# Gated rows that move into the places of the up projection's forms

## The chip, the cores and the metric

The kernel runs on one NeuronCore of a Trainium2 chip. The metric is the device time of one execution in microseconds; the kernel before takes 1738.56 us (median of 3 runs, 1738.2 to 1738.58). One execution was also recorded by the hardware profiler; every row below is from that one.

The engines are named as in the profile: PE is the matrix engine (PEld its weight loads), DVE the vector engine, ACT the scalar engine, POOL the general-purpose engine, and SP the queue that issues all DMA transfers here. Each engine works through its own list of instructions in order; semaphores tie the lists together.

## The reference

One step of a decoder layer is computed for 1024 prompt tokens and for 8 requests of 8 sample tokens, in float32: an RG-LRU branch and an S5 branch, merged, and then a ConvFFN. Only the ConvFFN bears on the change:

```python
h = modulate(x, p['g_norm2'], sh2, sc2)
up = h @ p['w_up']                              # 1024 -> 6144
uc, new_ffn_conv = causal_dwconv(ffn_conv, up, p['ffn_conv_w'], p['ffn_conv_b'])   # 3 taps
ua, ub = jnp.split(uc, 2, axis=-1)
x = x + gt2[:, None] * ((jax.nn.gelu(ua) * ub) @ p['w_down'])                      # 3072 -> 1024
```

## The kernel before

Channels lie on the 128 partitions, tokens along the free dimension. The tokens are in two halves: half 0 has the 64 sample tokens and 512 prompt tokens (576 columns), half 1 the other 512. Every operand of a float32 product is split into two parts that the matrix engine takes: the high part is a copy by ACT into the rounded type fp32r, the low part is a subtraction by DVE (value minus high part). A product is then three matmuls: high by high, high weight by low row, low weight by high row.

**The up projection** (`up`, L1451) takes the 6144 output channels in 12 column pairs b = 0 to 11, each with a part 0 (the gelu argument) and a part 1 (the factor). For each of these 24 steps a `Quad` makes seven block products `p1` to `p7` in place of eight, after Strassen and Winograd. Their moving operands are the *forms* B11, B21, B22, T1 to T4: sums and differences of the blocks of h, four tiles each, split once ahead of the loop and kept in SBUF for all 24 steps. B11, B21, T2, T4 and B22 lie in the 20 places P0 to P19 of the pool `pairs` (the table `FORMS` at L1133 gives the places), T1 and T3 in the pool `forms`. Product `p1` reads B11, `p2` B21, `p3` B22, `p4` T4, `p5` T1, `p6` T2 and `p7` T3. A step runs p1, then p4 of the step before it (`pend`), p5, p6, p2, p3, p7; the p4 of the last step comes after the loop. In the rows, L1238 is a product with 288-column matmuls (p1, p2, p6, p4), L1234 one with 512 columns (p3, p5), L1241 is p7.

A product leaves PSUM through `evac` (L1393 on ACT for p4, L1398 on DVE for p2, p3 and p7). When both halves of 128 channels are there, `finish` does the convolution: `fix` moves the carried columns on POOL (L1364 to L1369), L1374 (ACT) and two L1376 (DVE) are the three taps, L1483 multiplies prompt columns by the gelu and L1481 does the same for the 64 sample columns on POOL (tile `cs`). SP stores both to the DRAM tiles `act0` and `act1` (L1482, L1484).

**The down projection** follows. `down_a` (half 0) loads all 24 gated row blocks back with `load_act`: SP loads one into a buffer `al` (L1493), ACT and DVE split it into the tile `act` (L1147, L1148). Then `strip` goes over four strips of 256 output channels. In each, `weights` loads 12 pieces of `w_down` (L192), each split on ACT and DVE (L175, L176), and each piece meets two row blocks in 24 matmuls (L223). `down_b` does the same for half 1 (L1531).

**Buffers.** `al` shares the tag `cp` (five buffers) with `t1`, `p5` and `u2`, PSUM results of a Quad that wait for their second operand. Split weights `wh` and `wl` have three buffers each, raw weights eight. The `act` tiles are in a pool of 28 buffers that is opened only when the pools of the up projection, `pairs` among them, are closed; it takes over their memory, so that a first write to an `act` tile waits for whatever last used that memory.

**Order.** A scheduler orders the instructions of each engine by the program's order and by priorities. Code under `tc.high_priority(offset=n)` counts as n places earlier. SP issues in its own list's order: a transfer that waits holds back all behind it.

Of the kernel before, what the change touches and what calls it, by code (L numbers as in the profile page):

```python
# [8 lines left out]
F32 = mybir.dt.float32  # L9
F32R = mybir.dt.float32r  # L10
# [40 lines left out]
def _body(ctx, nc, tc, a):  # L51
# [4 lines left out]
    pairs = ctx.enter_context(ExitStack())  # L56
    pp = pairs.enter_context(tc.tile_pool(name="pairs", bufs=1))
    phase = ctx.enter_context(ExitStack())

    def pool(name, bufs=1):  # L60
        return phase.enter_context(tc.tile_pool(name=name, bufs=bufs, reuse_waits="tile"))
# [32 lines left out]
    def slot(i, name, dt=F32R):  # L94
        return pp.tile([128, 2, 576], dt, tag=f"P{i}", name=name)
# [5 lines left out]
    WID = (576, 512)  # L101
# [55 lines left out]
    def rg(name):  # L157
        return tmp("rg", [128, 604], name, bufs=4 if two else 7)
# [181 lines left out]
    def new_acc(name):  # L340
        return tmp("acc", [128, 512], name, bufs=1)
# [787 lines left out]
    actd = [dp.tile([24, 128, WID[h]], F32, name=f"act{h}") for h in range(2)]  # L1129
# [3 lines left out]
    FORMS = dict(B11=(12, 14, 8, 10), B21=(13, 15, 9, 11), T2=(0, 1, 2, 3), T4=(4, 5, 6, 7), B22=(16, 17, 18, 19))  # L1133
# [12 lines left out]
    def split_form(x, f):  # L1146
        S.activation(x[:, 0], f, AF.Copy)  # L1147
        V.tensor_sub(x[:, 1], f, x[:, 0].bitcast(F32))  # L1148
# [127 lines left out]
    def cpt(name):  # L1276
        return uw.tile([128, 576], F32, tag="cp", name=name, bufs=5)

    def blocks_of(w):
        q = Blocks(w)  # L1280
        with tc.high_priority(offset=300):
            q.load("A11", "A21", "A22", "A12")
            q.sums(V)
        return q
# [98 lines left out]
    def evac_up(b, part, gl):  # L1383
        m0 = 24 * part + 2 * b
        raw = {}

        def evac(i, half, y, z, e=None):
            t = tmp("rx", [128, 656], "up", bufs=5)
            o = t[:, 32:544] if half else t[:, :576]
            o = halves(o) if len(y.shape) == 3 else o  # L1390
            with tc.high_priority(offset=1000):
                if z is None:
                    S.activation(o, y, AF.Copy)  # L1393
                elif e is not None:
                    V.tensor_sub(o, y, z)
                    V.tensor_add(o, o, e)
                else:
                    V.tensor_add(o, y, z)  # L1398
            raw[i, half] = t
            if (i, 1 - half) in raw:  # L1400
                finish(i, raw, part, m0 + i, gl, 2 * b + i)

        return evac

    def up_lead():

        nonlocal rB2
        gl = {}
        Q = [Quad(q, evac_up(0, i, gl)) for i, q in enumerate(lead)]
        x = slot512(2, "wx")  # L1410
        Q.append(Quad(Blocks(a["w_up"][12], (("A11", x[:, 0]), ("A12", x[:, 1]))), evac_up(0, 1, gl)))
        Q[1].q.load("A11", "A12")
        Q[0].p1()
        rB2 = slot(3, "rstdB2", F32)[:, 0, :512]
        with tc.high_priority(offset=200):
            rstd_from(acc2, 512, "rstdB2", out=rB2)
            ST = h2b_load()
        Q[0].p2()
        Q[1].p1()
        Q[1].p2()  # L1420
        e = mm("e")
        ada_tail()
        h2b(ST)
        Q[0].p3_first(e[:, 0])
        with tc.high_priority(offset=300):
            Q[1].q.load("A21", "A22")
            Q[1].q.sums(G)
        Q[0].p5_last()
        Q[1].p3_first(e[:, 1])
        Q[1].p5_last()  # L1430
        for q in Q:
            q.p6()
            q.c12()
        for q in Q:
            q.p7()
        Q[0].p4()
        return Q[1]
# [13 lines left out]
    def up():  # L1451
        pend = up_lead()
        for b in range(1, 12):
            gl = {}
            for part in range(2):
                q = Quad(blocks_of(a["w_up"][12 * part + b]), evac_up(b, part, gl))
                q.p1()
                pend.p4()
                q.p5()
                q.p6()  # L1460
                q.p2()
                q.p3()
                q.p7()
                pend = q
        pend.p4()

    def finish(i, raw, part, m, gl, k):
        for half in range(2):
# [15 lines left out]
            nc.sync.dma_start(actd[half][k][:, 512 * half - 512:] if half else actd[0][k][:, 64:576], u[:, :512])  # L1484


    def load_act(half, k):
        n = WID[half]
        x = pp.tile([128, 2, 576], F32R, tag="act", name=f"act{half}_{k}", bufs=28)[:, :, :n]

        with tc.high_priority(offset=150 if half == 0 and k < 2 else 0):
            t = cpt("al")[:, :n]
            nc.sync.dma_start(t, actd[half][k])  # L1493
            split_form(x, t)
        return x

    def down_a():
        act = [load_act(0, k) for k in range(24)]
        acc3 = new_acc("acc3A")
        for b in range(4):  # L1500
            acc = strip(0, a["w_down"], b, act, 24)
            for j in range(2):
                m = 2 * b + j
                d = x2d[0][m * 128:(m + 1) * 128]
                x = load_x(d, "x2r")
                xo = rg("xo")[:, :512]
                with tc.high_priority(offset=400):
                    for y, c0, c1 in acc[j].p:
                        V.scalar_tensor_tensor(xo[:, c0:c1], y, modT[:, 40 + m, 0:1], x[:, c0:c1],
                                               op0=OP.mult, op1=OP.add)  # L1510
                resid_s(acc[j], 40 + m)
                acc_sq(acc3, xo, m == 0)
                nc.sync.dma_start(d, xo)
        hot.append(final(0, acc3, None, 0))

    def down_b():

        act = [load_act(1, k) for k in range(24)]
        X3 = [pp.tile([128, 2, 576], F32, tag="act", name=f"x3_{i}", bufs=28).rearrange("p r x -> p (r x)")[
            :, :1024].rearrange("p (r x) -> p r x", r=2) for i in range(4)]  # L1520
        acc3 = tmp("accb", [128, 512], "acc3B", bufs=1)
        CUT = 18

        def rows_of(T, b, k0, k1, tok):
            for i, (hi, lo) in enumerate(weights(a["w_down"], b, range(k0 // 2, k1 // 2))):
                for m in range(2):
                    c = slice(m * 128, (m + 1) * 128)
                    for k in range(2):
                        kb = k0 + 2 * i + k
                        for n, (y, r) in enumerate(((hi, 0), (hi, 1), (lo, 0))):  # L1530
                            T_.matmul(T[:, m, tok], y[:, k, c], act[kb][:, r, tok], start=kb + n == 0,  # L1531
                                      stop=kb == 23 and n == 2, skip_group_check=True)
                tick()

        def out(T, b, tok):
            for j in range(2):
                m = 2 * b + j
                x = load_x(x2d[1][m * 128:(m + 1) * 128, tok], "x2r")
                xo = X3[b][:, j, tok]
                with tc.high_priority(offset=400):  # L1540
                    V.scalar_tensor_tensor(xo, T[:, j, tok], modT[:, 40 + m, 0:1], x, op0=OP.mult, op1=OP.add)
                if b < 3:
                    acc_sq(acc3[:, tok], xo, m == 0)
                else:
                    sq.append(rg("sq")[:, tok])
                    S.activation(sq[-1], xo, AF.Square)
            if b < 3:
                scale_gf(X3[b][:, :, tok], b)

        def scale_gf(x, b):  # L1550
            for j in range(2):
                S.activation(x[:, j], x[:, j], AF.Copy, scale=v("gf")[:, 2 * b + j:2 * b + j + 1])

        whole = slice(0, 512)
        T = [mm("mm")]
        rows_of(T[0], 0, 0, 24, whole)
        out(T[0], 0, whole)
        for b in range(1, 4):
            T.append(mm("mm"))
            rows_of(T[b], b, 0, CUT, whole)  # L1560
        for t in range(2):
            tok = slice(256 * t, 256 * t + 256)
            sq = [acc3[:, tok]]
            for b in range(1, 4):
                rows_of(T[b], b, CUT, 24, tok)
                out(T[b], b, tok)
            g = final(1, sq, [x[:, :, tok] for x in X3], 512 + 256 * t, scale_gf)
            if t == 0:
                hot.append(g)
            else:  # L1570
                drain(g)
# [73 lines left out]
    ph = pool("forms")  # L1645
    tp = pool("up", 2)
    rB2 = None
    up()
    nc.sync.dma_start(a["o_sfc"], fconv)
    nc.sync.dma_start(a["o_pfc"], fcarry)  # L1650
    phase.close()
    pairs.close()

    pp = pool("act")
    tp, ph = pool("tmp2", 2), pool("part2")
    two = True
    down_a()
    down_b()


# [147 lines left out]
```

## Time and profile before

| | |
|---|---|
| median of 3 runs | 1738.56 us (1738.2 to 1738.58) |
| the profiled execution | 1742.4 us, its span 1740.6 us |
| PE busy | 1688.3 us, 97% of the span |
| DVE, ACT, POOL busy | 1198.6, 878.0, 220.7 us |
| granted TensorE clock, mean | 0.988 of full speed |
| HBM traffic | 143 GB/s over the span |

The span is the time from the first to the last instruction of the core; the rest of the profiled time lies around it. PE is busy almost throughout, so a place where it is idle, or where its clock is lowered, is time that the end of the program sees. The places are found by cutting the span into short windows, and then by the list of instructions in order of time in such a window, where each row says how long its engine was idle before it and what released it. The step from the up to the down projection lies between 1414 and 1440 us.

### The profile page before, as it was taken

How to read it: one execution, taken by the hardware profiler on the slowest of the kernel's cores; microseconds unless marked ns; L12 is line 12 of the kernel's file. 1: busy time of each engine (PE TensorE's matmuls, PEld its weight loads, DVE VectorE, ACT ScalarE, POOL GpSimd, SP SyncE). 2: the span in 40 equal slices, each digit the busy share in tenths (PEclk: the TensorE clock that was granted, in tenths of full speed). 3: DMA queues.
4: the chain of work that ended last, by engine and by line, in shares of the span. 5: the costliest groups of instructions: out<-in, count | busy, mean ns of one | idle time of the engine just before them, and what ended most of it. 6: DMA issues, size and time to landing. Idle time of an engine off the chain costs nothing.

```text
span 1740.6 us, 29344 instructions
## 1 busy us (share of the span) xinstructions
PE 1688.3 (97%) x10654; PEld 1521.1 (87%) x10654; DVE 1198.6 (69%) x2559; ACT 878.0 (50%) x1539; POOL 220.7 (13%) x488
## 2 busy tenths in 40 slices
PE   6999999999999999999998999999999989999997
PEld 2999999999997877788777999999999979999887
DVE  8878688956745686666669877777777766336426
ACT  4557668424534476744446555555555545234224
POOL 0012110100000001020021323322222230000000
PEclk8999999999999999999998999999999999999999
DMA  8375333467646655455662322222222249345634
GB/s 304 106 239 163 101 117 126 123 181 214 196 132 202 206 173 155 135 158 181 202 223 68 91 77 75 75 75 75 76 75 76 80 131 298 122 136 174 193 97 134
DMA packets 158993, 250.85 MB, mean 144 GB/s; under 512 B 34049, under 2 KB 57601, under 8 KB 158849
## 3 DMA queue, kind: packets, MB, share of 16 engines
q1 hardware_dynamic: 158848, 248.99, 45.8%
q8 instruction: 83, 1.36, 0.3%
q14 instruction: 62, 0.50, 0.1%
HBM read 205.20 MB, written 43.73 MB: 143 GB/s over the span
## 4 chain that ended last, share of the span: by engine, by line
PE 71%; DVE 6%; DMA 2%; ACT 1%; issue 1%; POOLq 0%; SPq 0%; POOL 0%; DVEq 0%; ACTq 0%
PE mm L225 15%; PE mm L223 15%; PE b L1238 13%; PE e L1234 8%; PE mm L1531 7%; PE a L1238 4%; PE b L1241 3%; PE sada L268 1%; DMA al<-act 1%; DVE wlo L176 1%; PE pv L777 1%; PE pg L951 1%; PE prs L347 0%; PE sx L707 0%; PE sx L708 0%
## 5 line engine op out<-in xcount | busy, mean ns | idle before, releaser
L176 DVE TENSOR_TENSOR wlo<-raw,whi 128x512 fp32r<-128x512 f32 x240 | 165.2, 688 | 163.9 <-ACT whi L175 131.2
L175 ACT ACTIVATE whi<-raw 128x512 fp32r<-128x512 f32 x240 | 150.6, 627 | 242.9 <-PE mm L225 101.5
L223 PE MATMUL mm<-h1A,whi 128*128 128x288 f32 x1024 | 184.3, 299 | 0.0
L225 PE MATMUL mm<-h1B,whi 128*128 128x512 f32 x512 | 163.7, 399 | 0.0
L176 DVE TENSOR_TENSOR wl<-raw,wh 128x512 fp32r<-128x512 f32 x105 | 72.1, 688 | 122.5 <-ACT wh L175 117.4
L223 PEld LDWEIGHTS mm<-h1A,whi 128*128 128x128 f32 x1024 | 152.2, 190 | 0.2
L223 PE MATMUL mm<-act,wh 128*128 128x288 f32 x768 | 136.2, 299 | 8.0 <-ACT act L1147 4.0
L1238 PE MATMUL b<-T,wh 128*128 128x288 f32 x768 | 135.9, 297 | 4.4 <-DVE T L1148 2.0
L175 ACT ACTIVATE wh<-raw 128x512 fp32r<-128x512 f32 x105 | 65.8, 629 | 144.0 <-PE mm L1531 82.2
L1531 PE MATMUL mm<-act,wh 128*128 128x512 f32 (+1 forms) x456 | 124.2, 360 | 0.0
L223 PEld LDWEIGHTS mm<-act,wh 128*128 128x128 f32 x768 | 114.1, 191 | 9.5 <-ACT act L1147 4.5
L1238 PEld LDWEIGHTS b<-T,wh 128*128 128x128 f32 x768 | 115.0, 190 | 8.0 <-DVE T L1148 2.9
L225 PEld LDWEIGHTS mm<-h1B,whi 128*128 128x128 f32 x512 | 93.5, 188 | 25.8 <-issue 4.5
L244 ACT ACTIVATE wh<-wA 128x512 fp32r<-128x512 f32 x94 | 59.3, 630 | 107.7 <-PE b L1238 42.0
L223 PE MATMUL mm<-h1A,wlo 128*128 128x288 f32 x512 | 111.0, 298 | 2.1 <-DVE wlo L176 2.1
L245 DVE TENSOR_TENSOR wl<-wA,wh 128x512 fp32r<-128x512 f32 x94 | 65.2, 694 | 55.7 <-ACT wh L244 55.1
L225 PE MATMUL mm<-h1B,wlo 128*128 128x512 f32 x256 | 100.5, 393 | 0.7 <-DVE wlo L176 0.7
L1531 PEld LDWEIGHTS mm<-act,wh 128*128 128x128 f32 x456 | 80.7, 188 | 14.9 <-issue 0.5
L1376 DVE SCALAR_TENSOR_TENSOR uc<-up,vec,uc 128x624 f32<-128x624 f32 (+1 forms) x96 | 75.8, 805 | 14.5 <-ACT uc L1374 11.4
L1376 DVE SCALAR_TENSOR_TENSOR gl<-up,vec,gl 128x624 f32<-128x624 f32 (+1 forms) x96 | 76.1, 804 | 13.8 <-ACT gl L1374 12.6
L223 PEld LDWEIGHTS mm<-h1A,wlo 128*128 128x128 f32 x512 | 83.0, 190 | 2.3 <-DVE wlo L176 2.3
L223 PE MATMUL mm<-act,wl 128*128 128x288 f32 x384 | 83.6, 299 | 0.2
(440 smaller groups left out, 4203.6 us busy)
## 6 DMA issues: line engine op xcount, KB each, us to landing
raw<-w_in SPq DMA_DIRECT2D x128, 256.0 KB, 2.7
raw<-w_down SPq DMA_DIRECT2D x105, 256.0 KB, 2.7
wA<-w_up SPq DMA_DIRECT2D x94, 256.0 KB, 2.7
adaw<-w_ada SPq DMA_DIRECT2D x56, 256.0 KB, 3.2
act<-uc SPq DMA_DIRECT2D x48, 256.0 KB, 2.1
araw<-w_ada SPq DMA_DIRECT2D x20, 512.0 KB, 7.8
s5a<-s5d SPq DMA_DIRECT2D x16, 512.0 KB, 4.0
raw<-w_rgp SPq DMA_DIRECT2D x32, 256.0 KB, 2.7
```

Source lines behind the costliest of these rows:

```text
L175: S.activation(hi, raw, AF.Copy)
L176: V.tensor_sub(lo, raw, hi.bitcast(F32))
L223: T_.matmul(T[m][:, h, :288], y[:, k, c], x[:, r, h * 288:(h + 1) * 288], **f)
L225: T_.matmul(T[0][:, m, tok], y[:, k, c], x[:, r, tok], **f)
L244: S.activation(hi, src, AF.Copy)
L245: V.tensor_sub(lo, src, hi.bitcast(F32))
L268: T_.matmul(sa[g:g + 32], cs[:, k], x, start=k < 4, stop=k >= 4)
L1234: T_.matmul(acc, w, x, **f)
L1238: T_.matmul(acc[:, h, :288], w, x[:, h * 288:(h + 1) * 288], **f)
L1241: T_.matmul(acc[:, h, o:o + 256], w, x[:, h * 256:(h + 1) * 256], **f)
L1376: V.scalar_tensor_tensor(dst, t[:, k:k + n], fw[:, k, m:m + 1], dst, op0=OP.mult, op1=OP.add)
L1531: T_.matmul(T[:, m, tok], y[:, k, c], act[kb][:, r, tok], start=kb + n == 0, stop=kb == 23 and n == 2, skip_group_check=True)
```

## The change

- The gated rows no longer have a pool of 28 buffers that opens after the up projection. Row blocks 0 to 19 of half 0 take the 20 places of `pairs`, in the order B11, B21, T2, B22, T4, the order in which these forms are last read (last p1, p6 and p2, p3, p4). Blocks 20 to 23, and blocks 0 to 3 of half 1, are in a new pool of 8 buffers, opened where the old one was; blocks 4 to 23 of half 1 take the 20 places again. `pairs` stays open.
- The first four `load_act` calls stand inside the last step of `up`, between its p3 and its p7, with a priority of 300. Before, the first two had 150, and all stood after `up`.

```diff
@@ up()
                 q.p2()
                 q.p3()
+                if (b, part) == (11, 1):
+                    with tc.high_priority(offset=300):
+                        act = [load_act(0, k) for k in range(4)]
                 q.p7()
                 pend = q
         pend.p4()
+        return act
...
+    PLACES = [FORMS[n][j] for n in ("B11", "B21", "T2", "B22", "T4") for j in range(4)]
+    xp = None
+
+    def more(name):
+        return xp.tile([128, 2, 576], F32R, tag="act", name=name, bufs=8)
+
     def load_act(half, k):
-        n = WID[half]
-        x = pp.tile([128, 2, 576], F32R, tag="act", name=f"act{half}_{k}", bufs=28)[:, :, :n]
-
-        with tc.high_priority(offset=150 if half == 0 and k < 2 else 0):
-            t = cpt("al")[:, :n]
-            nc.sync.dma_start(t, actd[half][k])
-            split_form(x, t)
+        n, j, name = WID[half], k - 4 * half, f"act{half}_{k}"
+        x = (slot(PLACES[j], name) if 0 <= j < 20 else more(name))[:, :, :n]
+        t = cpt("al")[:, :n]
+        nc.sync.dma_start(t, actd[half][k])
+        split_form(x, t)
         return x
 
-    def down_a():
-        act = [load_act(0, k) for k in range(24)]
+    def down_a(act):
+        act = act + [load_act(0, k) for k in range(4, 24)]
...
-    pairs.close()
-
-    pp = pool("act")
+
+    xp = pool("act")
```

What this does to the engines' lists is shown at three places. On PE, around the last p4 (`b<-T_0_10463` to `b<-T_3_10481`; `mm` are the two PSUM tiles of the first strip, which the two programs number differently). Before:

```order
L1241 MATMUL b<-T_3_10457,wl 128x256 x2
L1238 MATMUL b<-T_0_10463,wh 128x288 x4
...
L1238 MATMUL b<-T_3_10481,wl 128x288 x2
L223 MATMUL mm_16308<-act_0_16187,wh 128x288 x2
L223 MATMUL mm_16309<-act_0_16187,wh 128x288
```

and now:

```order
L1241 MATMUL b<-T_3_10457,wl 128x256 x2
L223 MATMUL mm_16307<-act_0_16091,wh 128x288 x4
L223 MATMUL mm_16307<-act_0_16091,wl 128x288 x2
L223 MATMUL mm_16307<-act_1_16096,wh 128x288 x4
L223 MATMUL mm_16307<-act_1_16096,wl 128x288
L1238 MATMUL b<-T_0_10463,wh 128x288 x4
...
L1238 MATMUL b<-T_3_10481,wl 128x288 x2
L223 MATMUL mm_16307<-act_1_16096,wl 128x288
L223 MATMUL mm_16308<-act_0_16091,wh 128x288 x4
```

Eleven matmuls on the first two row blocks now stand between p7 and the last p4. On DVE, from the evacuation of the last p2 (`up<-a`) on; `up<-e` is that of p3, `up<-b` that of p7, `wl<-raw` is a piece of `w_down`. Before:

```order
L1398 TENSOR_TENSOR up<-a,t_15922 128x576
...
L1398 TENSOR_TENSOR up<-b,p_15988 128x512
...
L1376 SCALAR_TENSOR_TENSOR uc<-up,vec,uc 128x512
L1483 TENSOR_TENSOR uc<-uc,gl 128x512 x2
L1148 TENSOR_TENSOR act_0_16187<-al,act_0_16187 128x576
L1148 TENSOR_TENSOR act_1_16192<-al,act_1_16192 128x576
```

and now, the first rows and then those from the third piece of weights on:

```order
L1398 TENSOR_TENSOR up<-a,t_15922 128x576
L1148 TENSOR_TENSOR act_0_16091<-al,act_0_16091 128x576
L1148 TENSOR_TENSOR act_1_16096<-al,act_1_16096 128x576
...
L1148 TENSOR_TENSOR act_5_16211<-al,act_5_16211 128x576
L1148 TENSOR_TENSOR act_6_16216<-al,act_6_16216 128x576
L176 TENSOR_TENSOR wl<-raw,wh 128x512
L1376 SCALAR_TENSOR_TENSOR uc<-up,vec,uc 128x624
L1376 SCALAR_TENSOR_TENSOR uc<-up,vec,uc 128x512
L1376 SCALAR_TENSOR_TENSOR uc<-up,vec,uc 128x624
L176 TENSOR_TENSOR wl<-raw,wh 128x512
L1487 TENSOR_TENSOR uc<-uc,gl 128x512
L1376 SCALAR_TENSOR_TENSOR uc<-up,vec,uc 128x512
L1148 TENSOR_TENSOR act_7_16221<-al,act_7_16221 128x576
```

All 24 subtractions stood behind the last convolution; now seven stand ahead of its last four taps, and the eighth behind them. On SP, from the first load on (`act_126` is the DRAM tile of half 0, `act_127` that of half 1). Before, with the last store of sample columns (`<-cs`):

```order
L1482 DMA act_126<-cs 128x64
L1484 DMA act_126<-uc 128x512
L1484 DMA act_127<-uc 128x512
L1093 DMA x2r<-x2d_117 128x512 x2
L1493 DMA al<-act_126 128x576 x10
```

and now, from the store before it to the same place:

```order
L1486 DMA act_126<-cs 128x64
L1502 DMA al<-act_126 128x576 x2
...
L1502 DMA al<-act_126 128x576 x2
L192 DMA raw<-w_down 128x512
L1486 DMA act_126<-cs 128x64
L192 DMA raw<-w_down 128x512
L1488 DMA act_126<-uc 128x512
L1502 DMA al<-act_126 128x576
L1488 DMA act_127<-uc 128x512
L1502 DMA al<-act_126 128x576 x11
```

Before, five of the 24 loads stood ahead of the last store of sample columns and 19 behind it; now twelve stand ahead and twelve behind.

## Rows read from the trace of the kernel before

**Rows 1.** Busy time by windows; the first row names the columns.
```profile
core 0: us, PE busy (x) PEld busy (x) DVE busy (x) ACT busy (x) POOL busy (x), PEclk, DMA share, GB/s
1431.00:1433.00 2.00, 0.80 (x3) 0.80 (x4) 2.00 (x4) 0.00 (x0) 2.00 (x1) 0.50 0.00 0
...
1437.00:1439.00 2.00, 2.00 (x17) 2.00 (x17) 0.00 (x0) 0.00 (x0) 0.00 (x0) 0.98 1.00 317
...
1440.00:1480.00 40.00, 38.34 (x273) 36.43 (x272) 26.75 (x44) 23.03 (x38) 0.00 (x0) 1.00 0.91 297
1480.00:1591.00 111.00, 111.00 (x835) 111.00 (x834) 44.23 (x78) 34.55 (x59) 0.00 (x0) 1.00 0.46 142
```

**Rows 2.** Timeline of PE: start us, duration us, instruction, in brackets idle before.
```profile
1419.45 0.40 PE L1241 MATMUL b<-T,wl 128*128 128x256 f32 x2
...
1421.56 0.77 PE L1238 MATMUL b<-T,wh 128*128 128x288 f32 x4 [1.71 <-DVE up L1398]
...
1428.55 0.67 PE L223 MATMUL mm<-act,wh 128*128 128x288 f32 x3 [3.56 <-ACT act L1147]
...
1432.20 0.85 PE L223 MATMUL mm<-act,wh 128*128 128x288 f32 x2 [2.99 <-DVE act L1148]
...
1437.26 0.69 PE L223 MATMUL mm<-act,wh 128*128 128x288 f32 x4
...
1591.50 0.63 PE L1531 MATMUL mm<-act,wh 128*128 128x512 f32 x2
```

**Rows 3.** Timeline of ACT: last p4's evacuation, first row blocks.
```profile
1425.34 0.63 ACT L1393 ACTIVATE up<-b 128x576 f32<-128x576 f32 x1
...
1427.83 2.96 ACT L1147 ACTIVATE act<-al 128x576 fp32r<-128x576 f32 x5
```

**Rows 4.** Timeline of DVE over the same stretch.
```profile
1414.20 0.76 DVE L1398 TENSOR_TENSOR up<-a,t 128x576 f32<-128x576 f32 x1 [0.94 <-PE a L1238]
...
1420.72 0.69 DVE L1398 TENSOR_TENSOR up<-b,p 128x512 f32<-128x512 f32 x1
...
1427.30 2.97 DVE L1376 SCALAR_TENSOR_TENSOR uc<-up,vec,uc 128x624 f32<-128x624 f32 x4 [1.14 <-ACT uc L1374]
...
1431.40 3.43 DVE L1148 TENSOR_TENSOR act<-al,act 128x576 fp32r<-128x576 f32 x5
```

**Rows 5.** Timeline of POOL: a sample product in mid-loop, the last carry, the last product.
```profile
1346.74 0.71 POOL L1481 TENSOR_TENSOR cs<-uc,gl 128x64 f32<-128x64 f32 x1 [2.01 <-DVE uc L1376]
...
1426.04 0.24 POOL L1364 COPY up<-up 128x64 f32<-128x64 f32 x1 [4.90 <-ACT up L1393]
...
1429.69 5.32 POOL L1481 TENSOR_TENSOR cs<-uc,gl 128x64 f32<-128x64 f32 x1 [2.30 <-DVE uc L1376]
```

**Rows 6.** Timeline of SP's issues.
```profile
1409.84 0.90 SPq L1493 DMA_DIRECT2D al<-act  x2
...
1414.99 0.32 SPq L1493 DMA_DIRECT2D al<-act  x1
...
1435.04 0.33 SPq L1482 DMA_DIRECT2D act<-cs  x1
...
1437.40 9.94 SPq L1493 DMA_DIRECT2D al<-act  x10
```

**Rows 7.** SP's own waits, 1405 to 1470: us in total, times, longest.
```profile
SPq L1482 <- POOL cs L1481: 7.2, 1, 7.2
```

**Rows 8.** Groups of instructions, 1405 to 1600: busy us, mean ns | idle before.
```profile
L175 ACT ACTIVATE wh<-raw 128x512 fp32r<-128x512 f32 x54 | 33.7, 627 | 67.1 <-PE mm L223 56.4 <-PE mm L1531 5.4 <-PE b L1238 4.5
L1148 DVE TENSOR_TENSOR act<-al,act 128x576 fp32r<-128x576 f32 x24 | 17.5, 755 | 11.3 <-ACT act L1147 11.2
...
L1147 ACT ACTIVATE act<-al 128x576 fp32r<-128x576 f32 x24 | 15.6, 679 | 16.2 <-DMA al<-act 16.0
...
L1374 ACT ACTIVATE uc<-up,vec 128x624 f32<-128x624 f32 x2 | 1.8, 908 | 1.5 <-POOL up L1364 1.5
```

**Rows 9.** Loads of row blocks, least, median and longest.
```profile
DMA to landing us min/median/max: 2.7/3.8/5.8
```

More of the change, by code (lines that the diff above doesn't have):

```diff
@@ L1518, in down_b @@
         act = [load_act(1, k) for k in range(24)]
-        X3 = [pp.tile([128, 2, 576], F32, tag="act", name=f"x3_{i}", bufs=28).rearrange("p r x -> p (r x)")[
+        X3 = [xp.tile([128, 2, 576], F32, tag="act", name=f"x3_{i}", bufs=8).rearrange("p r x -> p (r x)")[
             :, :1024].rearrange("p (r x) -> p r x", r=2) for i in range(4)]
@@ L1647, in _body @@
     rB2 = None
-    up()
+    act = up()
     nc.sync.dma_start(a["o_sfc"], fconv)
@@ L1651, in _body @@
     phase.close()
-    pairs.close()
-    pp = pool("act")
+    xp = pool("act")
     tp, ph = pool("tmp2", 2), pool("part2")
     two = True
-    down_a()
+    down_a(act)
     down_b()
```

## The prediction

> **What bounds the kernel now.** I first read the page: PE is busy 97% of the span, so the question is only where the other 3% lie, and whether the change touches them. Cutting the span into windows shows it: from 1480 us to the end of the first half of the down projection 835 matmuls of 288 columns take 111 us, 0.133 us each and none lost, while 1440 to 1480 holds 273 (36.3 us of work in 40, 3.7 lost), and from 1431 to 1433 the granted clock is 0.50, the lower of the two levels (1.2 GHz), and from 1437 to 1439 0.98 [rows 1]. The timeline of PE gives the rest: it waits 1.71 us for DVE ahead of the last p4, 3.56 us for ACT ahead of the first row block, 2.99 us for DVE three matmuls later [rows 2].
>
> The whole loss follows from two ends. The last p7 ends at 1419.45 + 0.40 = 1419.85, the second half starts at 1591.50 [rows 2]: 171.65 us. In it lie p4 (24 matmuls) and the first half (4 strips x 24 blocks x 12 = 1152), 1176 x 0.133 = 156.4 us. So 15.2 us are lost, and that is the most that this change can give. They are the three waits, 8.3 us; the lower clock, 24 matmuls in 0.67 + (1437.26 - 1432.20) = 5.73 us in place of 3.2, so 2.5 us; 3.7 us from 1440 to 1480; and 0.7 us of small gaps.
>
> Why the waits are there is read on the other engines. The first copy of a row block on ACT starts at 1427.83, although its load left at 1409.84 [rows 3, 6]: it stands behind the evacuation of the last p4 at 1425.34 and the convolution that follows, and its memory is free only when the old pools are. On DVE all subtractions stand behind eight taps and four products; the first starts at 1431.40 [rows 4]. And after five row blocks both engines run dry, for SP issues the next ten loads only at 1437.40: it waited 7.2 us for the last `cs` on POOL, which took 5.32 us and ended with DVE's series of operations on two SBUF operands (1431.40 + 3.43 = 1434.83) [rows 4 to 7].
>
> **The change, part by part.** I follow the new order from 1414.20, up to which the rows of before hold.
>
> *The wait of 1.71 us ahead of p4: gone.* DVE's `up<-b`, which p4 waits for, was the ninth row after 1414.20 and still is: one tap, one product and a tap's place went to three subtractions. At 0.69 us per DVE row (five subtractions in 3.43 us, [rows 4]) it starts at 1414.20 + 9 x 0.69 = 1420.4 and ends near 1421.1; before, 1420.72 to 1421.41. PE meanwhile has 11 matmuls on blocks 0 and 1 (1.46 us): their loads left at 1409.84 [rows 6] and land by 1413.7 at the median of 3.8 [rows 9], the splits are done with DVE's third row, at 1416.3, the first piece of `w_down` with its seventh, at 1419.0. So PE runs from 1419.85 to 1421.3 and into p4 without a gap. If the first splits were late, p4 would be late with them, since PE takes its list in order; the splits have over 2 us in hand. Value 0, from 0 to 1 us.
>
> *The waits of 3.56 and 2.99 us and the lower clock: gone at this place.* p4 ends at 1421.3 + 3.2 = 1424.5; then 13 matmuls remain of blocks 0 and 1, to 1426.2. Blocks 2 to 5 are split by then or in time: DVE reaches the third piece of weights at 1421.1 + 6 x 0.69 = 1425.2, and block 6 by 1428.0. PE has 48 matmuls for blocks 2 to 5, to 1432.6.
>
> *A new wait at block 7.* ACT's next tap (L1374) waits for POOL's L1364, which moves carries of the p4 evacuation. Before, that copy had 0.24 us [rows 5]. Now DVE runs without a pause from the third weights through block 6, and I take it that POOL gets its turn only then, at 1428.0. The tap takes 0.91 and the copy of the fourth piece of weights 0.63 [rows 8]: 1429.8, its subtraction 1430.5; then seven DVE rows to block 7's low part, 1430.5 + 7 x 0.69 = 1435.3. PE needs it at 1432.6 + 8 x 0.133 = 1433.7. So 1.6 us are lost, from 0 (POOL gets in between, all 1.8 us earlier) to 3 (DVE at the 0.755 of [rows 8] and one more row late).
>
> *A new wait at block 12.* Twelve loads now stand ahead of the last `cs`, so PE has work on to block 11: 16 matmuls more for blocks 6 and 7 from 1435.3, then 48, which is 1437.4 and 1443.8. The loads from block 12 on still stand behind `cs`, and that behind DVE's next pause. DVE has block 7, one product, the sixth weights, blocks 8 to 11 and the seventh weights, whose buffer PE frees at 1437.4; it pauses at 1440.1. Then `cs` 0.33, three issues of 0.33 to 0.4 ahead of the load, which leaves at 1441.5 and lands after 2.7 to 3.8 us [rows 9], copy 0.68, subtraction 0.755 [rows 8]. The high part is there at 1444.9 to 1446.0 against 1443.8, the low part costs 0.5 more: 1.6 to 2.7 us. I take 2.2; it is 0 if `cs` passes at once, and 4.8 at the longest landing of 5.8.
>
> *Slips up to 1480.* Of the 3.7 us lost there I keep 1.5: the loads now start in a stretch in which the DMA had pauses (share 0.00 from 1431 to 1433, [rows 1]), but from block 13 on they still go through five buffers at about 1 us each (ten in 9.94 us, [rows 6]) while PE takes 1.6 us per block. From 0.5 to 3.7.
>
> *At nothing:* the order of places itself. Each form's last product is over before its place is written (B11's four products before), the number of loads and splits is the same, and half 1 waits for the same blocks' last reader as before. If a place were freed late, its split would wait on ACT with all behind it; the covers are these four products and, for blocks 16 to 19 in T4's places, the 19 us and more from p4's end to their use. 0, up to 0.7 us for one subtraction that now stands between the evacuations of the first strip.
>
> *Sum:* 0 + 0 + 1.6 + 2.2 + 1.5 = 5.3 us lost where 15.2 were, a gain of 9.9, say 10. The profiled execution takes 1742.4, so 1732.4; it is 3.8 us above the median of the runs, 1738.56, and I take the same difference from that: **1728.6 us**.
>
> **A rule weighed against the trace.** The row: the last `cs` took 5.32 us under back-to-back DVE operations and ended 0.2 us after the last; in mid-loop it took 0.71 [rows 5]. The Trainium skill, "SBUF — State Buffer", section "Who interferes with whom", says that a DVE instruction with two SBUF inputs contends with a GpSimd one that reads SBUF, and that who issues first holds the pair "for the whole instruction". By that the turn would pass at the end of one DVE instruction, as 0.71 would fit; 5.32 over seven does not. I go by the longer row; the other is the second case below.
>
> **The rivals.**
>
> *POOL gets its turn after one DVE row.* Speaks for it 0.71 us in mid-loop; against it 5.32 in this very place [rows 5]. Then L1364 ends at 1426.1, block 7 is split at 1433.5 in place of 1435.3, and the last `cs` passes near 1433, so that block 12's load lands by 1438.5. Both new waits go, 1.5 us stay: 13.7 gained, 1724.9 us. That is the result by the rule above, too.
>
> *The new waits grow until the clock falls again.* Before, 3.56 us idle, three matmuls and 2.99 us idle were enough. With the longest landing, 1441.5 + 5.8 + 0.68 + 0.755 = 1448.7, 4.9 us late, plus the 2.5 us of clock, 1.6 and 1.5: 10.5 lost, 4.7 gained, 1733.9 us. For it: that landing is in the trace [rows 9]. Against: it is the longest, and PE has 8 us of work between the two waits.
>
> *The strip is bound by its loads, so that an earlier start is given back.* For it: the DMA is busy 0.91 from 1440 to 1480 [rows 1]. The eighth load after 1437.40, block 12's, left near 1444.4; now it leaves at 1441.5. If the strip's end moves only by that and some slack, 3 us: 1735.6 us, no change that counts. Against: 1 us per load and 1.6 us of PE per block.
>
> *Slower: the last `cs` is kept waiting while DVE finds work.* SP's list stops behind it, and each us past 1441 goes straight to the end once PE has run out at 1443.8. Loads 12 on would be split 6 us after `cs`. With 2.5 us of clock lost as well, the gain is spent when `cs` ends at 1447, and beyond 1451 the kernel is slower by over 0.2%; at 1454 it would be near 1745. For it: the 7.2 us that SP waited [rows 7]. Against: DVE's next row is block 12 itself, whose load is behind `cs`; so DVE must pause, and by then it has nothing else.
>
> **How the numbers follow.** Forecast (7 to 12.5 us gained) 0.62; POOL in turn 0.13; clock falls again 0.14; given back 0.07; slower 0.04. 0.2% is 3.5 us, about what a measurement of this kernel can tell from no change. Faster by more: 0.62 + 0.13 + 0.14 = 0.89; same 0.07; slower 0.04. The range takes the forecast's bounds and most of the two cases beside it: 1724.2 (the first rival and a little more) to 1735.0.
>
> **What would show it.** Right: no idle PE row of over 0.5 us between 1419 and 1432; 11 matmuls of L223 ahead of the last L1238; clock 1.00 from 1425 to 1440; a wait of 1 to 3 us at block 7 for DVE and another at block 12 for the load, with `cs` shortly ahead of it on SP; L1531 starting near 1581.5. Wrong: a second stretch at 0.50; L1364 done at 1426.1 and no wait at block 7 (first rival); L1531 at 1588 or later with PE waiting for loads in 1440 to 1480 (given back); SP waiting for POOL beyond 1447 (slower).

## The result and the profile after

The changed kernel takes 1729.53 us (median of 4 runs, 1726.55 to 1731.12) against 1738.57 us of the kernel before (4 runs, 1738.2 to 1740.44): a ratio of 0.9936 with a 95% interval of 0.9922 to 0.9949, 9 us less. The profiled execution is the slowest of the four, 1731.12 us with a span of 1729.3 us.

First the timeline of PE over the stretch that the prediction cut out (start, duration, engine, line, operation, out<-in, shape, count, and in brackets the idle time ahead and what ended it).

```profile
1417.76 0.40 PE L1241 MATMUL b<-T,wl 128*128 128x256 f32 x2
...
1419.33 0.29 PE L223 MATMUL mm<-act,wl 128*128 128x288 f32 x1
1419.59 0.80 PE L1238 MATMUL b<-T,wh 128*128 128x288 f32 x4
...
1435.94 0.55 PE L223 MATMUL mm<-act,wh 128*128 128x288 f32 x2 [1.19 <-DVE act L1148]
...
1465.07 0.77 PE L223 MATMUL mm<-act,wh 128*128 128x288 f32 x4 [1.91 <-DVE rs L1099]
...
1580.25 0.62 PE L1540 MATMUL mm<-act,wh 128*128 128x512 f32 x2
```

The three waits of [rows 2] are gone. 11 matmuls on row blocks stand ahead of the last p4, and PE enters p4 without a pause. Two waits are new, 1.19 us at row block 8 and 1.91 us at the change from the first strip to the second. The last p7 ends at 1417.76 + 0.40 = 1418.16 and the second half starts at 1580.25: 162.09 us where there were 171.65, so 9.6 us come from this stretch. Of these 162.09 us, 156.4 are matmuls; 5.7 are lost.

The profiled executions differ by 1742.40 - 1731.12 = 11.3 us. The other 1.7 us lie ahead of the stretch (the last p7 ends 1.69 us earlier). They aren't shown to be the change's: in two more profiles of a kernel in which nothing ahead of that product was changed (before again, and before with its last `cs` on DVE) it ends at 1418.55 and at 1415.62, as the table of the experiments shows.

Next the windows, the same columns as [rows 1]: busy time and count of PE, PEld, DVE, ACT and POOL, then the granted clock, the DMA share and GB/s.

```profile
1431.00:1433.00 2.00, 2.00 (x17) 1.93 (x16) 1.63 (x3) 0.47 (x1) 0.00 (x0) 1.00 0.99 353
1437.00:1439.00 2.00, 2.00 (x17) 2.00 (x16) 2.00 (x4) 0.20 (x2) 0.00 (x0) 1.00 0.95 292
1440.00:1480.00 40.00, 38.09 (x275) 37.88 (x274) 20.41 (x36) 16.63 (x28) 0.00 (x0) 0.96 0.80 266
1466.00:1468.00 2.00, 2.00 (x11) 2.00 (x10) 2.00 (x7) 1.15 (x2) 0.00 (x0) 0.57 0.93 315
1468.00:1470.00 2.00, 2.00 (x11) 2.00 (x11) 0.51 (x1) 0.00 (x0) 0.00 (x0) 0.57 0.87 262
```

From 1431 to 1433 the clock is now full, and the DMA is busy where it stood still before. But behind the second new wait the clock falls, to 0.57: 24 matmuls take 4.8 us (1465.07 to 1469.85) in place of 3.2. So the 5.7 us are 1.2 (block 8), 1.9 (strip change), 1.6 (clock) and 1.0 of small gaps.

Why there is no long wait for POOL any more stands in POOL's timeline, which answers to [rows 5].

```profile
1424.47 0.24 POOL L1364 COPY up<-up 128x64 f32<-128x64 f32 x1 [5.12 <-ACT up L1393]
1424.78 0.54 POOL L1366 COPY vec<-up 128x16 f32<-128x16 f32 x1
1425.26 0.71 POOL L1368 COPY up<-fcarry 128x2 f32<-128x2 f32 x1
...
1429.50 1.32 POOL L1485 TENSOR_TENSOR cs<-uc,gl 128x64 f32<-128x64 f32 x1 [1.47 <-DVE uc L1376]
```

The carries take up to 0.7 us each, about one DVE operation, and the last `cs` 1.32 us where it took 5.32. DVE is busy all the while, first in a window over the carries and then in its rows over the last `cs`:

```profile
1425.00:1427.00 2.00, 2.00 (x17) 2.00 (x16) 2.00 (x4) 2.00 (x4) 1.88 (x4) 1.00 0.76 297
```
```profile
1429.34 0.68 DVE L176 TENSOR_TENSOR wl<-raw,wh 128x512 fp32r<-128x512 f32 x1
1429.94 0.68 DVE L1487 TENSOR_TENSOR uc<-uc,gl 128x512 f32<-128x512 f32 x1
1430.54 0.82 DVE L1376 SCALAR_TENSOR_TENSOR uc<-up,vec,uc 128x512 f32<-128x512 f32 x1
```

So POOL is let in between DVE's operations here. The prediction took it that POOL waits until DVE pauses.

The wait at block 8 is read on three engines. SP first (its issues answer to [rows 6], its wait to [rows 7]):

```profile
1428.05 0.34 SPq L1659 DMA_DIRECT2D o_pfc<-fcarry  x1
1428.49 1.73 SPq L1502 DMA_DIRECT2D al<-act  x2
...
1430.84 0.33 SPq L1486 DMA_DIRECT2D act<-cs  x1
...
1435.95 10.80 SPq L1502 DMA_DIRECT2D al<-act  x11
```
```profile
SPq L1659 <- POOL fcarry L1369: 1.8, 1, 1.8
...
SPq L1486 <- POOL cs L1485: 0.5, 1, 0.5
```

Then ACT:

```profile
1432.53 1.44 ACT L1147 ACTIVATE act<-al 128x576 fp32r<-128x576 f32 x2 [3.85 <-DMA al<-act]
1433.88 1.14 ACT L175 ACTIVATE wh<-raw 128x512 fp32r<-128x512 f32 x2
```

And DVE:

```profile
1434.52 0.69 DVE L176 TENSOR_TENSOR wl<-raw,wh 128x512 fp32r<-128x512 f32 x1 [1.89 <-ACT wh L175]
1435.13 2.76 DVE L1148 TENSOR_TENSOR act<-al,act 128x576 fp32r<-128x576 f32 x4
```

Read from the end: PE waits for the subtraction of block 8, the first of the four at 1435.13. It needs nothing that is late itself, but in DVE's list it stands behind the subtraction of the sixth piece of weights, and that behind ACT's copy of it. ACT has the copies of blocks 10 and 11 in front of that copy, whose loads left only at 1428.49, behind the store of the carries, at which SP stood 1.8 us. The first of them had landed when ACT began, 4.0 us after it left. How much of the 1.19 us is the store's is a question for the runs below.

The wait at the strip change is read in DVE's timeline there, of the changed kernel and then of the kernel before.

```profile
1461.44 1.36 DVE L1148 TENSOR_TENSOR act<-al,act 128x512 fp32r<-128x512 f32 x2 [5.15 <-ACT act L1147]
1462.71 0.68 DVE L176 TENSOR_TENSOR wl<-raw,wh 128x512 fp32r<-128x512 f32 x1
1463.32 0.68 DVE L1148 TENSOR_TENSOR act<-al,act 128x512 fp32r<-128x512 f32 x1
1463.92 0.87 DVE L1518 SCALAR_TENSOR_TENSOR xo<-mm,modT,x2r 128x224 f32<-128x224 f32 x2
1464.71 0.21 DVE L1099 TENSOR_TENSOR rs<-mm,modT 128x64 f32<-128x64 f32 x1
```
```profile
1468.98 0.69 DVE L1148 TENSOR_TENSOR act<-al,act 128x512 fp32r<-128x512 f32 x1 [4.91 <-ACT act L1147]
...
1470.19 2.20 DVE L1148 TENSOR_TENSOR act<-al,act 128x512 fp32r<-128x512 f32 x3
1472.30 2.09 DVE L176 TENSOR_TENSOR wl<-raw,wh 128x512 fp32r<-128x512 f32 x3
1474.97 0.88 DVE L1509 SCALAR_TENSOR_TENSOR xo<-mm,modT,x2r 128x224 f32<-128x224 f32 x2 [0.58 <-PE mm L223]
```

A strip of half 0 ends with an evacuation on DVE (L1518, L1099; before, L1509), and the next strip needs the PSUM that it frees. Blocks of half 1 (the shape 128x512) stand ahead of it on DVE in both kernels, four of them before and three now. Before, they were done while PE still worked on the strip, and DVE waited 0.58 us for PE. Now the strip ends at 1465.07 - 1.91 = 1463.16, some 12 us earlier, but the splits of half 1 start only 7.5 us earlier (1461.44 for 1468.98), and PE waits for DVE.

### The profile page after: what moved, and what is told of

It is laid out like the page before. It is cut to its first block, busy times and chain, and to the rows that moved or that the text cites. A ratio compares the mean times of both kernels' runs of the same rounds, so it can differ in the third digit from the quotient of the medians.

```text
span 1729.3 us, 29328 instructions
## 1 busy us (share of the span) xinstructions
PE 1683.5 (97%) x10654; PEld 1517.8 (88%) x10654; DVE 1198.7 (69%) x2559; ACT 877.0 (51%) x1539; POOL 221.5 (13%) x488
## 4 chain that ended last, share of the span: by engine, by line
PE 72%; DVE 6%; DMA 2%; ACT 1%; issue 1%; POOL 0%; SPq 0%; DVEq 0%; ACTq 0%
PE mm L225 17%; PE mm L223 15%; PE b L1238 12%; PE mm L1540 7%; PE e L1234 7%; PE a L1238 4%; PE b L1241 3%; DMA al<-act 1%; PE sada L268 1%; PE pv L777 1%; PE pg L951 1%; DVE wlo L176 0%; PE prs L347 0%; PE sx L707 0%; PE sx L708 0%
## 5 line engine op out<-in xcount | busy, mean ns | idle before, releaser
L1376 DVE SCALAR_TENSOR_TENSOR gl<-up,vec,gl 128x624 f32<-128x624 f32 (+1 forms) x96 | 76.1, 804 | 13.8 <-ACT gl L1374 12.6
L1376 DVE SCALAR_TENSOR_TENSOR uc<-up,vec,uc 128x624 f32<-128x624 f32 (+1 forms) x96 | 76.0, 805 | 12.2 <-ACT uc L1374 10.3
```

The source lines that it names most:

```text
L1376: V.scalar_tensor_tensor(dst, t[:, k:k + n], fw[:, k, m:m + 1], dst, op0=OP.mult, op1=OP.add)
```

## The experiments

All runs, with the stretch from the end of the last p7 to the start of the second half, of which 156.4 us are matmuls. The experiments ran on two chips, each beside the kernel before on the same chip (1740.88 us for places only, places reversed, half 1's places and stores later; 1740.71 us for the others).

| kernel | median us (runs) | ratio to before, 95% | last p7 ends | stretch | PE's waits |
|---|---|---|---|---|---|
| before | 1738.57 (4) | | 1419.85 | 171.65 | 1.71, 3.56, 2.99, 0.44, 0.26, 0.79 |
| before, profiled again | 1740.55 (1) | | 1418.55 | 170.85 | 1.71, 3.56, 2.57, 0.56, 0.26, 0.27 |
| changed | 1729.53 (4) | 0.9936 (0.9922 to 0.9949) | 1418.16 | 162.09 | 1.19, 1.91 |
| changed, again | 1730.05 (6) | 0.9934 (0.9919 to 0.9949) | 1415.91 | 159.47 | 0.87, 1.16 |
| places only | 1735.46 (10) | 0.9972 (0.9963 to 0.9981) | 1418.80 | 168.26 | 9.35 |
| places reversed | 1732.54 (4) | 0.9952 (0.9938 to 0.9966) | 1418.63 | 162.64 | 1.70, 2.50, 1.07 |
| half 1's places | 1725.71 (4) | 0.9916 (0.9902 to 0.9929) | 1415.40 | 157.78 | 0.37 |
| stores later | 1729.67 (5) | 0.9932 (0.9918 to 0.9945) | 1416.31 | 162.36 | 0.23, 2.91 |
| both of these | 1724.85 (5) | 0.9915 (0.9899 to 0.9930) | 1416.08 | 157.51 | 0.20 |
| before, last `cs` on DVE | 1735.83 (5) | 0.9967 (0.9953 to 0.9980) | 1415.62 | 167.62 | 1.70, 3.55, 3.12 |

PE's waits are all those that the timeline shows in the stretch. The end of the last p7 moves by 4.2 us between the kernel before and the same with its last `cs` on DVE (1419.85 and 1415.62), in which nothing ahead of it was changed. The stretch is therefore the better measure of what is done in it. It is not fixed either: it differs by 0.8 us between the two profiles of before and by 2.6 us between those of the changed kernel, so that the change gives 8.8 to 12.2 us by these four. What follows the stretch, from the start of the second half to the end of the span, takes 149.1 us in every one of the ten profiles.

### The places without the early loads

From the changed kernel, the loads go back behind `up`, with the old priorities:

```diff
-                if (b, part) == (11, 1):
-                    with tc.high_priority(offset=300):
-                        act = [load_act(0, k) for k in range(4)]
...
+        with tc.high_priority(offset=150 if half == 0 and k < 2 else 0):
...
-        act = act + [load_act(0, k) for k in range(4, 24)]
+        act = [load_act(0, k) for k in range(24)]
```

> The rows take the places of the forms, but all 24 load_act calls stand after up() again, the first two with a priority of 150, as before. If the places alone bring the gain (the splits need no longer wait for the old pools), this is as fast as the changed kernel, near 1729.5 us. If the four calls inside the last step are needed, since without them the order on DVE puts block 2's subtraction behind block 8's, PE waits at block 2: by that order some 20 rows of 0.69 us after 1420, near 1433 in place of 1426, 7 us of idle PE and then the lower clock, 2 us: near 1737 to 1739 us. I expect the second.

Measured: 1735.46 us, 5.4 us less than before and some 5 to 6 more than the changed kernel. PE again enters p4 without a wait, but then:

```profile
1435.22 0.85 PE L223 MATMUL mm<-act,wh 128*128 128x288 f32 x2 [9.35 <-DVE act L1148]
```

With the splits of only blocks 0 and 1 preferred, the scheduler puts block 2's subtraction ninth among those in DVE's list, behind block 8's, and PE, which takes the blocks in order, stands 9.35 us for it. DVE's row at that time:

```profile
1433.75 2.75 DVE L1148 TENSOR_TENSOR act<-al,act 128x576 fp32r<-128x576 f32 x4
```

Block 2's is the second of these four, done near 1435.1. The second case came true, but the time is lower than its 1737 to 1739 us: the wait is 9.35 us where 7 were expected, and the clock does fall behind it (0.50 from 1434 to 1438), but the changed kernel's own later waits of 1.19 and 1.91 us and its 1.6 us of lower clock aren't there, which the expectation had left in. So both halves of the change count: the places take away the wait for the old pools' memory, and the early loads of blocks 2 and 3 see to it that what is split next is what PE needs next.

### The places in the reverse order

```diff
-    PLACES = [FORMS[n][j] for n in ("B11", "B21", "T2", "B22", "T4") for j in range(4)]
+    PLACES = [FORMS[n][j] for n in ("T4", "B22", "T2", "B21", "B11") for j in range(4)]
```

> The same change with the places in the reverse order of their last products (T4, B22, T2, B21, B11). If the order of places is what lets the first splits go ahead of the last p4, blocks 0 to 3 now wait for the end of that p4 itself: the 1.7 us wait ahead of p4 is back, then copy and subtraction, 1.5 us, and the subtractions of blocks 4 on behind the taps: 4 to 6 us slower than the changed kernel, 1734 to 1736 us. If only the earlier loads on SP matter, within 1 us of 1729.5.

Measured: 1732.54 us, 2.5 to 3 us above the changed kernel, and a stretch only 0.5 us longer, so less than expected. The waits are those of a first block that has to wait for T4's last reader, p4:

```profile
1420.33 0.77 PE L1238 MATMUL b<-T,wh 128*128 128x288 f32 x4 [1.70 <-DVE up L1398]
...
1433.19 0.53 PE L223 MATMUL mm<-act,wh 128*128 128x288 f32 x2 [2.50 <-DVE act L1148]
...
1467.60 0.76 PE L223 MATMUL mm<-act,wh 128*128 128x288 f32 x4 [1.07 <-DVE rs L1099]
```

The wait ahead of p4 is back at its 1.7 us. These first two waits are 4.2 us where the changed kernel has 1.19. But the strip change costs 1.07 us in place of 1.91 and the clock stays full in this profile, which gives 2.4 us back. Against the changed kernel's second profile (below), which waits 1.16 us at the strip change with the clock full as well, the stretch is 3.2 us longer, as the medians have it. The waits that the order takes away are shown by the trace. A gain in time is likely but not clear of the spread: the intervals, 0.9938 to 0.9966 and 0.9922 to 0.9949, overlap.

### Half 1 waits for its own places

In the changed kernel blocks 0 to 3 of half 1 lie in the new pool, which is free at once, so that their loads and splits come in the middle of the first strip. Here block k of half 1 takes place k, and the new pool keeps its last four:

```diff
-        n, j, name = WID[half], k - 4 * half, f"act{half}_{k}"
+        n, j, name = WID[half], k, f"act{half}_{k}"
```

> Blocks 0 to 19 of half 1 take the 20 places and 20 to 23 the pool of 8, so that no block of half 1 is split before the last strip of half 0. Theory: the wait of 1.9 us at the change from the first strip to the second, and 1.6 us of lower clock behind it, come from three subtractions of half 1 that stand on DVE ahead of the evacuation, with loads that land late; both go, 3.5 us less than the changed kernel: 1726 us, and a narrower spread of the runs. Rival: the evacuation itself is late (its x2r load, or the raw weights), then the wait stays and the time is 1729.5 within 1 us.

Measured: 1725.71 us; the stretch is 157.78 us, 4.3 less than in the changed kernel's first profile and 1.7 less than in its second. DVE at the strip change now has the evacuation first, and waits for PE there:

```profile
1456.63 0.88 DVE L1518 SCALAR_TENSOR_TENSOR xo<-mm,modT,x2r 128x224 f32<-128x224 f32 x2 [0.56 <-PE mm L223]
1457.43 0.21 DVE L1099 TENSOR_TENSOR rs<-mm,modT 128x64 f32<-128x64 f32 x1
```
```profile
1432.55 0.53 PE L223 MATMUL mm<-act,wh 128*128 128x288 f32 x2 [0.37 <-DVE act L1148]
```

The second row, of PE, is the only wait left in the stretch. So the wait at the strip change, and the clock behind it, came from the early splits of half 1, as read from the trace. The later splits cost nothing further on, where the 149.1 us of the second half are the same. In the medians the gain is 3 to 4 us, with intervals that overlap (0.9902 to 0.9929, and 0.9922 to 0.9949 for the changed kernel). That block 8 too waits less (0.37 for 1.19) was not expected, and SP still stands at the store of the carries:

```profile
SPq L1659 <- POOL fcarry L1369: 1.8, 1, 1.8
```

### The output stores later

```diff
-    nc.sync.dma_start(a["o_sfc"], fconv)
-    nc.sync.dma_start(a["o_pfc"], fcarry)
...
+    nc.sync.dma_start(a["o_sfc"], fconv)
+    nc.sync.dma_start(a["o_pfc"], fcarry)
```

The two stores, one of which waited 1.8 us for POOL on SP, go behind the first half of the down projection in the program.

> The stores of the carries (o_sfc, o_pfc) are issued after down_a's code in place of before it. Theory: the wait of 1.2 us at block 8 is there because ACT has the copies of blocks 10 and 11 ahead of the sixth piece of weights, and their loads stood on SP behind o_pfc, which waited 1.8 us for POOL's last carry; then blocks 10 and 11 load 1.8 us earlier and the wait goes: 1.2 us less than the changed kernel, 1728.3 us. Rival: these loads are held by the buffers and the DMA, busy at 1.00 there; then the wait stays at 1 us or more.

Measured: 1729.67 us, no change against the changed kernel. PE shows why:

```profile
1433.37 0.53 PE L223 MATMUL mm<-act,wh 128*128 128x288 f32 x2 [0.23 <-DVE act L1148]
...
1463.47 1.25 PE L223 MATMUL mm<-act,wh 128*128 128x288 f32 x4 [2.91 <-DVE rs L1099]
```

The wait at block 8 goes down to 0.23 us, but this doesn't show that the store was its cause, for with half 1's places it was 0.37 with the store where it stood. SP's load of block 10 and ACT's copy of it are here:

```profile
1424.35 0.99 SPq L1502 DMA_DIRECT2D al<-act  x2
```
```profile
1429.96 1.44 ACT L1147 ACTIVATE act<-al 128x576 fp32r<-128x576 f32 x2 [2.90 <-DMA al<-act]
```

Counted from the end of the last p7, the load leaves at 8.0 us, where it left at 10.3 and 10.1 in the two profiles of the changed kernel and at 10.5 with half 1's places. But the copy starts at 13.7 us, against 14.4, 14.0 and 13.7. So the load left 2 us earlier and was there 0.4 to 0.7 us earlier, since it now took 5.6 us in place of 4.0. The rival, that these loads are held by the buffers and the DMA, is not ruled out, and what the store by itself costs stays open. What is won at block 8 is lost again at the strip change: the first strip is over earlier still, and the evacuation stands behind the same three splits of half 1. The four matmuls that took 0.77 us take 1.25: the granted clock is 0.51 from 1463.5 to 1465.5.

### Both together

> Both edits: half 1 in the places from its block 0 on, and the stores of the carries later. The first took 4.3 us from the stretch between the last p7 and the second half (157.8 against 162.1 us), of which 156.4 are matmuls. What is left there, 1.4 us, is 0.4 at block 8 and small gaps. Theory: 157.2 to 157.8 us in that stretch, the time within 0.6 us of half 1 in the places alone, 0.990 to 0.992 of before. Rival: the second edit, which alone changed nothing in the median, moves loads behind the last sample store and costs what it gives: 0.992 to 0.994.

Measured: 1724.85 us, a ratio of 0.9915 (0.9899 to 0.9930) to the kernel before; PE has one wait of 0.20 us in the whole stretch, 157.51 us long, of which 1.1 are lost. It is the fastest version here, but its runs (1723.5 to 1729.29) overlap those with the places of half 1 alone (1724.07 to 1728.21): the second edit's own gain isn't shown once the first is made.

### The changed kernel again

> The changed kernel once more, beside the others on one chip. A ratio near 0.9936 to before. If the wait at the change of strips depends on when the loads of half 1 land, its length differs from execution to execution, and the runs spread over some 4 us, from 1726 to 1731; if it is fixed, 1.9 us and the lower clock behind it are there again and the spread is that of before.

Measured: 1730.05 us, 1725.39 to 1731.70 over six runs; the profiled execution takes 1726.27 us. Its two waits are the same ones, but shorter, and the matmuls behind the second are hardly slower:

```profile
1433.35 0.53 PE L223 MATMUL mm<-act,wh 128*128 128x288 f32 x2 [0.87 <-DVE act L1148]
...
1461.70 0.77 PE L223 MATMUL mm<-act,wh 128*128 128x288 f32 x4 [1.16 <-DVE rs L1099]
```
```profile
1462.00:1464.00 2.00, 2.00 (x17) 2.00 (x16) 2.00 (x8) 1.58 (x4) 0.00 (x0) 1.00 1.06 290
```

The clock stays full. The stretch is 2.6 us shorter than in the first profile: 1.1 us of waits and 1.6 of clock. So two executions of one kernel differ here in the length of a wait and in whether the clock falls behind it. How much of the spread of the runs (6 us) this makes isn't shown; the twelve runs of the kernel before on this chip spread by 7.7 us.

### The kernel before, with its last `cs` on DVE

```diff
-                G.tensor_mul(two4(s8(c)), useg(u), useg(g))
+                (V if k == 23 else G).tensor_mul(two4(s8(c)), useg(u), useg(g))
```

> The kernel before, with the product of the sample columns of the very last row block on DVE in place of POOL (about 0.2 us of DVE). It asks what the 7.2 us that SP waited for POOL cost by themselves. Theory: the loads from the sixth on leave 4 to 5 us earlier, but PE's waits of 1.7, 3.6 and 3.0 us and the lower clock stay, since the first splits still stand behind the last convolution; only the slips after 1437 shrink: 1 to 3.5 us less than before, 0.998 to 0.9994. Rival: SP's wait is the cause of most of the loss, then 8 us or more are gained, 0.995 or less.

Measured: 1735.83 us, and a stretch of 167.62 us, 3.2 to 4.0 less than in the two profiles of before. On DVE the product takes 0.2 us, SP's ten loads leave at 1428.82, and the three waits of before stay. The median is 4.9 us below that of before on its chip, more than the 1 to 3.5 us of the theory and less than the 8 of the rival.

```profile
1417.32 0.77 PE L1238 MATMUL b<-T,wh 128*128 128x288 f32 x4 [1.70 <-DVE up L1398]
...
1424.30 0.67 PE L223 MATMUL mm<-act,wh 128*128 128x288 f32 x3 [3.55 <-ACT act L1147]
1428.10 0.85 PE L223 MATMUL mm<-act,wh 128*128 128x288 f32 x2 [3.12 <-DVE act L1148]
```

So the long `cs` on POOL cost the kernel before the losses behind 1437, some 3 to 4 us, and not the three waits. Those were the memory's and the order's, which the change removes.

### The kernel before again

> The kernel before, profiled once more. Theory 1: the last sample product on POOL takes 5.3 us again, since DVE's series of nine operations stands ahead of its turn each time. Theory 2: it takes 0.7 to 1.4 us as in mid-loop and in the changed kernels, and the long one was one execution's; then the wait of SP is shorter and the stretch from the last p7 to the second half is 1 to 4 us shorter than 171.65.

```profile
1428.41 5.32 POOL L1481 TENSOR_TENSOR cs<-uc,gl 128x64 f32<-128x64 f32 x1 [2.30 <-DVE uc L1376]
```

The `cs` of 5.32 us is there a second time, to the hundredth, and so is SP's wait of 7.2 us. It is no accident of one execution.

## Why the prediction was right, and where it wasn't

The predicted 1728.6 us stands against 1729.53, and 5.3 us lost in the stretch against 5.7 in the first profile of the changed kernel and 3.1 in the second. The total is right and the removal of the old losses is right; the losses that stay are others than those forecast.

- *The wait ahead of p4: gone.* As predicted, with 11 matmuls in front of it. It ran as worked out.
- *The two waits of 3.56 and 2.99 us and the low clock behind them: gone.* As predicted; the clock is 1.00 from 1431 to 1439.
- *A new wait at block 7, 1.6 us: it wasn't there* (0.1 us at most: block 7's first matmuls take 0.80 in place of 0.69). The step that failed is "POOL gets its turn only then, at 1428.0", which is 1426.3 in this profile, 1.69 us earlier than before at the last p7. L1364 starts at 1424.47 and takes 0.24 us, and the rows behind it 0.5 to 0.7 each with DVE busy. The first rival was right on this. It had more for it than the one row of 0.71 us: the 24 such products of the kernel before have a median of 1.04 us. The Trainium skill, "SBUF — State Buffer", section "SBUF: two separate sides", says that of a DVE operation with two SBUF inputs and a GpSimd operation that reads SBUF the one that starts first gets the shared pair "for the whole instruction". The copies of 0.5 to 0.7 us beside DVE operations of 0.68 to 0.87 agree with that; the last `cs` agrees less, since its 1.32 us are more than one such operation and the 0.34 us of the shortest `cs` in this trace, and the 5.32 us of before do not agree.
- *A new wait at block 12, 2.2 us: it wasn't there.* The same step: `cs` was over at 1430.8 and not at 1440, so SP went on.
- *Slips up to 1480, 1.5 us:* about 1.0 of small gaps are left.
- *"0, up to 0.7 us for one subtraction that now stands between the evacuations of the first strip", for the order of places:* this is the term that was too small. It looked at whether a place is freed in time, which holds. It didn't ask what DVE's list holds at the strip change once the strip ends 12 us sooner. Three subtractions, not one, came ahead of the first evacuation: 1.9 us of wait and 1.6 us of clock. The run with half 1 in its own places takes both away, so this cause is shown.
- *The wait at block 8, 1.2 us,* was not in the sum at all. It comes from the copies of blocks 10 and 11, which stand on ACT ahead of weights that are needed sooner and wait for their loads. The store of the carries on SP, past which the loads were moved, holds them back; the prediction counted `cs` there and not this store. How much of the wait is the store's stays open: it is 0.87 us in the changed kernel's second profile, 0.23 with the stores later and 0.37 with half 1's places alone.

So the forecast's 1.6 + 2.2 + 1.5 were replaced by 0.1 + 1.2 + 1.9 + 1.6 + 0.9. That the sums agree is partly luck; in the second profile, with 3.1 us lost, they do not. With POOL in turn, the first rival's 1724.9 us would have been the consequent forecast, and the version without the strip change's wait, 1725.71 us, comes within 1 us of it. The rivals of a given-back start and of a slower kernel have nothing for them: the start moved to 1580.25, and SP waited 0.5 us for `cs`. The clock did fall a second time, as another rival had it, but at another place and for 1.6 us.

What stays open: why POOL was shut out for 5.32 us in the kernel before, twice, when in the changed one it passes in one or two DVE operations. The DVE rows beside it are alike in kind (series of two-operand operations of 0.6 to 0.8 us without a pause), and mainly their order differs. With the places reversed, the product took 0.77 us in the same place, behind L1376 and beside two L1487. No run here tells what decides it.

## What to carry to other kernels

When a stage is made to start earlier, go through the in-order lists of the engines behind it and ask what else becomes ready at the old times and now stands ahead of something needed sooner: here loads of the next half, harmless before, held up a PSUM evacuation. A buffer that is free early is not a gain in itself; making the next half wait for its place took the wait and the lower clock away, 1.7 to 4.3 us of the stretch. And if an edit takes away a wait and gains nothing, look at the next wait in line: with the stores moved, the time went to the strip change. Whether such an edit pays once that wait is gone too has to be measured; here it isn't shown.

## What the runs showed of the hardware

- POOL's small operations passed between DVE's without a pause of DVE, at 0.24 to 1.32 us each, in the changed kernel; in the kernel before one took 5.32 us, in both of its profiles.
- The length of one wait did not alone decide whether the granted clock fell: behind a wait of 1.91 us (changed kernel) it was 0.57, behind 2.50 us (places reversed, at 1433) two matmuls took 0.53 us, as they do after a short wait (0.37 us, half 1's places), and the clock was 1.00, as here:

```profile
1433.00:1435.00 2.00, 1.81 (x13) 1.81 (x14) 2.00 (x4) 0.00 (x0) 0.00 (x0) 1.00 1.04 353
```
